# Recurrent layer: all blocks finished ahead of the output projections, and part of the elementwise work on GpSimd

## The chip, the cores and the metric

One core of a Trainium2 chip runs the whole program. The metric is the device time of one execution in microseconds, as the median of several runs.

## What is computed

Four layers, each a mixer and a squared-ReLU MLP with a residual and a layer norm, over 256 positions of 1024 features, all in float32. The mixers are a retention layer, a gated recurrent layer, an attention layer and a second retention layer. The change is in the recurrent one, layer 1:

```
gate_branch, rec = split(x @ w_in, 2)
gate_branch = gelu(gate_branch)
u = causal conv of width 4 over rec, + conv_b
r = sigmoid(blockwise u @ w_a + b_a);  i = sigmoid(blockwise u @ w_x + b_x)
log_a = -8 * r * softplus(-lam);  a = exp(log_a)
b_in = sqrt(-expm1(2 * log_a)) * (i * u)
h[t] = a[t] * h[t-1] + b_in[t]
out = (h * gate_branch) @ w_o
```

Its width is 1280, and the kernel takes it as 5 blocks of 256.

## The kernel before

Every float32 product is made of three matmuls on operands that are split into a high part (rounded to the matmul's format) and a low part (the rest): high x high, high x low, low x high (`mm3`, L145). Weights come in chunks of 1 MB. `chunk` (L122) loads one by a single DMA from SyncE's queue into one of 3 `raw` buffers and splits it into one of 5 `hl` buffers, in two halves of 1024 columns: for each, ScalarE casts the high part (L142, CAST) and VectorE subtracts for the low part (L143, TENSOR_TENSOR). A `raw` buffer is free for the next load when both halves are subtracted. An `hl` buffer is free when its matmuls are done. Activations are split in the same way. `self.hold` places low halves behind a layer norm's last step.

In the recurrent layer (`lru`, L527) the order of the work is written out by hand; a scheduler of the framework then settles the order on each engine, which the program keeps when it runs. Chunks come through a `Feed` that makes each two ahead of its use: four of `rec`, the gate weights of blocks 0 to 2, the last `rec`, then gate branch 0, the gate weights of blocks 3 and 4, gate branches 1 to 4 ("b" below) and the five projection loads ("o"). Each block n goes through these steps:
- `conv` (L569) makes U[n] from the projection in PSUM: ScalarE writes it, VectorE adds three shifted products for each half (L575). It is split into uT.
- `gates` (L579): matmuls on uT, four ScalarE functions for each half, and four VectorE steps that leave B[n] (the decay), Q[n] and U[n] (L591 to L594).
- `roots` (L607): ScalarE takes the square root of Q[n].
- `scan` (L612): VectorE multiplies U[n] by Q[n] (L613) and runs the recurrence in two scans (L615) from B[n] and U[n] into Q[n].
- `gate_branch` (L617): 48 matmuls into PSUM. Those of blocks 3 and 4 lie in two of the four work banks.
- `finish` (L621): ScalarE's gelu of the gate branch into `gg`, VectorE's product with Q[n] (L624), and the split of the product into YT[n], by ScalarE (L142) and VectorE (L143). YT has 3 buffers.
- `out` (L631): 24 matmuls of YT[n] with the projection's weights, into four accumulators.

With three buffers for YT, blocks 0 and 1 are finished right after their scans, and blocks 2, 3 and 4 behind the projections of blocks 0 and 1 (L676 to L681). `close` (L297) then does the projections of blocks 2 to 4 and the layer norm.

Of the kernel before, what the change touches and what calls it, by code (L numbers as in the profile page):

```python
# [9 lines left out]
F32 = mybir.dt.float32  # L10
F32R = mybir.dt.float32r
# [87 lines left out]
class Model:  # L99
# [19 lines left out]
        return [[self.acc.tile([128, 512], F32, name=f"acc{t}{n}", tag=f"acc{t}{n}") for n in range(2)]  # L119
                for t in range(2)]  # L120

    def chunk(self, src, k, n, pieces=2, loads=1, hold=True, mid=None):  # L122

        nc = self.nc
        raw = self.raw.tile([128, 2048], F32, name="raw", tag="raw")
        hl = self.hl.tile([128, 2, 2048], F32R, name="hl", tag="hl")
        w = k * n
        src = src.rearrange("p k n -> p (k n)")
        step = w // loads
        for a in range(0, w, step):  # L130
            nc.sync.dma_start(out=raw[:, a:a + step], in_=src[:, a:a + step])
            if mid and a == 0:
                mid()
        step = w // pieces
        for a in range(0, w, step):
            lo = self.split(hl[:, 0, a:a + step], hl[:, 1, a:a + step], raw[:, a:a + step])
            if hold and self.hold:
                self.after(lo, self.hold)
        return hl[:, :, :w].rearrange("p s (k n) -> p s k n", n=n)

    def split(self, hi, lo, x):
        self.nc.scalar.copy(out=hi, in_=x)  # L142
        return self.nc.vector.tensor_sub(out=lo, in0=x, in1=hi.bitcast(F32))  # L143

    def mm3(self, out, st, mv, start, stop):  # L145

# [380 lines left out]
    def lru(self, l, final):  # L527
        nc, mm, A, tc = self.nc, self.nc.tensor.matmul, self.A, self.tc
# [3 lines left out]
        act = nc.scalar.activation  # L532
        with tc.tile_pool(name="lru", bufs=1) as p:
            UT, GB, YT = {}, {}, {}
            U = [p.tile([128, 2, 256], F32, name=f"U{n}") for n in range(5)]
            Q = [p.tile([128, 2, 256], F32, name=f"Q{n}") for n in range(5)]
            B = [p.tile([128, 2, 256], F32, name=f"B{n}") for n in range(5)]
            last = {}

            def load(n, o, hold=True):  # L540
                return self.chunk(win[o + n], 8, 256, hold=hold)

            def block(ps, w):
                for b in range(2):
# [65 lines left out]
                last["s"] = m  # L610

            def scan(n):  # L612
                nc.vector.tensor_mul(out=U[n], in0=U[n], in1=Q[n])  # L613
                for b in range(2):
                    nc.vector.tensor_tensor_scan(out=Q[n][:, b], data0=B[n][:, b], data1=U[n][:, b], initial=0.0, op0=ALU.mult, op1=ALU.add)  # L615

# [4 lines left out]
            def finish(n):  # L621
                g = p.tile([128, 2, 256], F32, name="gg", tag="gg", bufs=2)
                self.after(act(out=g, in_=GB[n], func=AF.Gelu_apprx_tanh), last["s"])
                nc.vector.tensor_mul(out=g, in0=g, in1=Q[n])  # L624
                YT[n] = p.tile([128, 2, 2, 256], F32R, name="yT", tag="yT", bufs=3)
                self.split(YT[n][:, 0], YT[n][:, 1], g)

            def out_load(n):
                return self.chunk(wo[n], 2, 1024)

            def out(n, w, t, ns=(0, 1)):  # L631
                c = slice(t * 128, t * 128 + 128)
# [32 lines left out]
            w = feed(("b", 3))  # L665
            for n in range(5):
                roots(n)
            for n in range(5):
                scan(n)
                if n < 2:  # L670
                    finish(n)
            gate_branch(3, w)
            gate_branch(4, feed(("b", 4)))
            acc = self.accs()
            gb = self.ln_load(l, 0)
            for n in range(2):  # L676
                w = feed(("o", n))
                out(n, w, 0)
                out(n, w, 1)
                finish(n + 2)  # L680
            finish(4)  # L681
            self.close(acc, gb, final, [lambda t, ns, n=n: out(n, feed(("o", n)), t, ns) for n in (2, 3, 4)])


# [371 lines left out]
```

## Time and profile before

| | us |
|---|---|
| median of 3 runs (1320.05 to 1322.92) | 1321.05 |
| the profiled execution | 1322.59 |
| its span, first to last instruction | 1320.8 |
| TensorE busy | 1303.6 |
| VectorE busy | 956.6 |
| ScalarE busy | 658.9 |
| GpSimd busy | 26.0 |

In the rows PE is TensorE, DVE VectorE, ACT ScalarE and POOL GpSimd; L12 is line 12 of the kernel. Times in the rows below count from the start of the span, in microseconds. A row of a timeline is one instruction, or several that follow each other on the same line (x2 and so on, the whole time of the group). An instruction's time includes the end of its pipeline, so that the next one on its engine starts a little before it is over. What stands in square brackets is the idle time ahead of an instruction and what ended it. The granted clock is a share of TensorE's full speed.

### The profile page before, as it was taken

To read this page: it belongs to the slowest core of one execution; us is meant where nothing else is said; L and a number is where in the kernel's file an instruction comes from. 1 tells how busy PE (TensorE), PEld (TensorE's weight loads), DVE (VectorE), ACT (ScalarE), POOL (GpSimd) and SP (SyncE) were. 2 spreads that over 40 slices of the span, in tenths; PEclk is the share of its full clock that TensorE was granted. 3 is DMA by queue.
4 is the path that set the end of the run, shared out by engine and by line. 5 is a ranking of instruction groups with operands and counts; after the bars stand their busy time and mean duration, and the time that the engine had idled before them with its cause. 6 is when DMAs were issued, how large, how long until landed. Compare 5 with 4: busy or idle time off the path is not lost.

```text
span 1320.8 us, 17993 instructions
## 1 busy us (share of the span) xinstructions
PE 1303.6 (99%) x7130; PEld 1130.1 (86%) x7130; DVE 956.6 (72%) x1490; ACT 658.9 (50%) x1026; POOL 26.0 (2%) x40
## 2 busy tenths in 40 slices
PE   9999999999999999999999999999999999999997
PEld 6888888888889978888888888888898888888886
DVE  6976678766678988666589886666786657876664
ACT  5654445444438945444357554444444445454440
POOL 0000000000000000000010000000000000000000
PEclk9999999999999999999999999999999999999999
DMA  7745544655544366555435365555554544465540
GB/s 286 285 163 191 187 164 160 225 193 190 193 159 166 128 238 240 191 192 191 151 114 203 130 237 192 191 191 192 186 206 174 188 156 177 154 236 189 194 143 32
DMA packets 37281, 243.59 MB, mean 184 GB/s; under 512 B 4311, under 2 KB 4812, under 8 KB 10188
## 3 DMA queue, kind: packets, MB, share of 16 engines
q1 hardware_dynamic: 37196, 242.43, 51.8%
q8 instruction: 56, 0.92, 0.3%
q14 instruction: 29, 0.24, 0.1%
HBM read 241.36 MB, written 1.05 MB: 184 GB/s over the span
## 4 chain that ended last, share of the span: by engine, by line
PE 90%; DVE 5%; ACT 3%; issue 1%; DMA 0%; SPq 0%; POOL 0%; DVEq 0%; POOLq 0%; ACTq 0%
PE wk L960 14%; PE acc L148 12%; PE acc L150 12%; PE acc L149 12%; PE wk L148 10%; PE wk L150 10%; PE wk L149 10%; PE wk L962 8%; DVE hl L143 2%; PE wk L266 1%; ACT hl L142 1%; PE wk L428 1%; DMA raw<-ret_vg 0%; PE wk L984 0%; DVE Q L615 0%
## 5 line engine op out<-in xcount | busy, mean ns | idle before, releaser
L143 DVE TENSOR_TENSOR hl<-raw,hl 128x1024 fp32r<-128x1024 f32 (+3 forms) x448 | 526.3, 1196 | 176.8 <-ACT hl L142 173.8
L142 ACT CAST hl<-raw 128x1024 fp32r<-128x1024 f32 (+3 forms) x448 | 447.0, 1033 | 307.7 <-PE acc L150 174.1
L148 PE MATMUL acc<-hl,hT 128*128 128x512 f32 x512 | 200.5, 392 | 0.0
L149 PE MATMUL acc<-hl,hT 128*128 128x512 f32 x512 | 200.1, 391 | 0.0
L150 PE MATMUL acc<-hl,hT 128*128 128x512 f32 x512 | 199.2, 389 | 0.0
L960 PE MATMUL wk<-xT,hl 128*128 128x512 f32 x832 | 197.6, 390 | 0.0
L960 PEld LDWEIGHTS wk<-xT,hl 128*128 128x128 f32 x832 | 155.9, 188 | 32.3
L148 PE MATMUL wk<-hl,xT 128*128 128x512 f32 (+1 forms) x432 | 159.0, 368 | 0.3 <-ACT xT L142 0.3
L149 PE MATMUL wk<-hl,xT 128*128 128x512 f32 (+1 forms) x432 | 157.0, 364 | 0.2 <-DVE hl L143 0.2
L150 PE MATMUL wk<-hl,xT 128*128 128x512 f32 (+1 forms) x432 | 157.0, 364 | 0.0
L948 ACT COPY tb<-wk 128x256 f32<-128x256 f32 x104 | 38.8, 373 | 156.3 <-PE wk L962 156.3
L150 PEld LDWEIGHTS acc<-hl,hT 128*128 128x128 f32 x512 | 96.1, 188 | 20.3
L148 PEld LDWEIGHTS acc<-hl,hT 128*128 128x128 f32 x512 | 96.3, 188 | 18.5
L149 PEld LDWEIGHTS acc<-hl,hT 128*128 128x128 f32 x512 | 96.3, 188 | 17.9
L962 PEld LDWEIGHTS wk<-xT,hl 128*128 128x128 f32 x832 | 106.7, 191 | 4.1
L962 PE MATMUL wk<-xT,hl 128*128 128x256 f32 x832 | 107.9, 283 | 0.0
L949 DVE TENSOR_TENSOR s<-wk,tb 128x256 f32<-128x256 f32 x104 | 44.1, 424 | 80.5 <-ACT tb L948 76.8
L148 PEld LDWEIGHTS wk<-hl,xT 128*128 128x128 f32 x432 | 81.7, 189 | 14.8 <-ACT xT L142 2.6
L150 PEld LDWEIGHTS wk<-hl,xT 128*128 128x128 f32 x432 | 81.6, 189 | 14.0 <-DVE xT L143 1.6
L149 PEld LDWEIGHTS wk<-hl,xT 128*128 128x128 f32 x432 | 81.9, 190 | 12.8 <-DVE hl L143 1.1
L150 PE MATMUL wk<-xT,hl 128*128 128x256 f32 x288 | 81.6, 284 | 0.1
L148 PE MATMUL wk<-xT,hl 128*128 128x256 f32 x288 | 81.5, 283 | 0.0
(231 smaller groups left out, 1786.0 us busy)
## 6 DMA issues: line engine op xcount, KB each, us to landing
raw<-mlp SPq DMA_DIRECT2D x64, 1024.0 KB, 4.8
raw<-mlp_1b SPq DMA_DIRECT2D x56, 1024.0 KB, 4.8
raw<-ret_vg SPq DMA_DIRECT2D x30, 1024.0 KB, 4.8
raw<-ret_qk SPq DMA_DIRECT2D x16, 1024.0 KB
raw<-ret_o SPq DMA_DIRECT2D x16, 1024.0 KB, 5.0
raw<-lru_in SPq DMA_DIRECT2D x10, 1024.0 KB, 4.8
raw<-mlp_1a SPq DMA_DIRECT2D x8, 1024.0 KB
raw<-lru_o SPq DMA_DIRECT2D x5, 1024.0 KB, 4.7
```

The source lines that it names most:

```text
L142: self.nc.scalar.copy(out=hi, in_=x)
L143: return self.nc.vector.tensor_sub(out=lo, in0=x, in1=hi.bitcast(F32))
L148: mm(out, lhsT=st[0], rhs=mv[0], start=start, stop=False)
L149: mm(out, lhsT=st[0], rhs=mv[1], start=False, stop=False)
L150: mm(out, lhsT=st[1], rhs=mv[0], start=False, stop=stop)
L266: nc.tensor.transpose(ps[:, k * 128:k * 128 + 128], self.h[t][:, (j * 4 + k) * 128:(j * 4 + k + 1) * 128], self.idn)
L428: nc.tensor.transpose(tp[:, b * 128:b * 128 + 128], Y[h, t][:, b * 128:b * 128 + 128], self.idn)
L948: nc.scalar.copy(out=tb, in_=ps_lo)
L949: nc.vector.tensor_add(out=s, in0=ps_hi, in1=tb)
L960: mm(ps[b], lhsT=w[:, 0, k, f], rhs=xT[:, k], start=k == 0, stop=False)
L962: mm(ps[b][:, 256:], lhsT=w[:, 1, k, f], rhs=xT[:, k, 0], start=False, stop=k == 7)
```

## The change

The second half of a chunk's low part can be made by GpSimd (`pool=True`); it is, for the five gate-branch loads (o == 0 in `load`) and the five projection loads. GpSimd also does U*Q of blocks 1 to 4. U and B of a block become halves of one tile, UB, and YT takes its buffer from the same five slots: a block's yT is written where its U and B were. All five blocks are scanned and finished ahead of the projections, and gate branches 3 and 4 are written ahead of the scans. The lines of the changed kernel are three further on in these functions.

```
-    def chunk(self, src, k, n, pieces=2, loads=1, hold=True, mid=None):
+    def chunk(self, src, k, n, pieces=2, loads=1, hold=True, mid=None, pool=False):
...
-            lo = self.split(hl[:, 0, a:a + step], hl[:, 1, a:a + step], raw[:, a:a + step])
-            if hold and self.hold:
+            by = nc.gpsimd if pool and a + step == w else None
+            lo = self.split(hl[:, 0, a:a + step], hl[:, 1, a:a + step], raw[:, a:a + step], by)
+            if hold and self.hold and not by:
                 self.after(lo, self.hold)
...
-    def split(self, hi, lo, x):
+    def split(self, hi, lo, x, by=None):
         self.nc.scalar.copy(out=hi, in_=x)
-        return self.nc.vector.tensor_sub(out=lo, in0=x, in1=hi.bitcast(F32))
+        return (by or self.nc.vector).tensor_sub(out=lo, in0=x, in1=hi.bitcast(F32))
...
-            U = [p.tile([128, 2, 256], F32, name=f"U{n}") for n in range(5)]
+            UB = [p.tile([128, 2, 2, 256], F32, name="UB", tag="UB", bufs=5) for n in range(5)]
+            U, B = [x[:, 0] for x in UB], [x[:, 1] for x in UB]
             Q = [p.tile([128, 2, 256], F32, name=f"Q{n}") for n in range(5)]
-            B = [p.tile([128, 2, 256], F32, name=f"B{n}") for n in range(5)]
...
-                return self.chunk(win[o + n], 8, 256, hold=hold)
+                return self.chunk(win[o + n], 8, 256, hold=hold, pool=o == 0)
...
-                nc.vector.tensor_mul(out=U[n], in0=U[n], in1=Q[n])
+                (nc.gpsimd if n else nc.vector).tensor_mul(out=U[n], in0=U[n], in1=Q[n])
...
-                YT[n] = p.tile([128, 2, 2, 256], F32R, name="yT", tag="yT", bufs=3)
+                YT[n] = p.tile([128, 2, 2, 256], F32R, name="yT", tag="UB", bufs=5)
...
-                return self.chunk(wo[n], 2, 1024)
+                return self.chunk(wo[n], 2, 1024, pool=True)
...
+            gate_branch(3, w)
+            gate_branch(4, feed(("b", 4)))
             for n in range(5):
                 scan(n)
-                if n < 2:
-                    finish(n)
-            gate_branch(3, w)
-            gate_branch(4, feed(("b", 4)))
+                if n:
+                    finish(n - 1)
+            finish(4)
...
                 out(n, w, 1)
-                finish(n + 2)
-            finish(4)
```

What this does to the engines' queues is seen at three places. VectorE from the first U*Q to block 0's finished low part, before (U0 to U4, Q0 to Q4 and B0 to B4 are the blocks' tiles, gg_4143 and yT_4146 those of block 0, gg_4152 that of block 1):

```order
L613 TENSOR_TENSOR U0_3391<-U0_3391,Q0_3396 128x512
L613 TENSOR_TENSOR U1_3392<-U1_3392,Q1_3397 128x512
L615 SCALAR_TENSOR_TENSOR Q0_3396<-B0_3401,U0_3391 128x256 x2
L615 SCALAR_TENSOR_TENSOR Q1_3397<-B1_3402,U1_3392 128x256 x2
L613 TENSOR_TENSOR U2_3393<-U2_3393,Q2_3398 128x512
L613 TENSOR_TENSOR U3_3394<-U3_3394,Q3_3399 128x512
L624 TENSOR_TENSOR gg_4143<-gg_4143,Q0_3396 128x512
L624 TENSOR_TENSOR gg_4152<-gg_4152,Q1_3397 128x512
L615 SCALAR_TENSOR_TENSOR Q2_3398<-B2_3403,U2_3393 128x256 x2
L143 TENSOR_TENSOR yT_4146<-gg_4143,yT_4146 128x512
```

The same place on VectorE afterwards (hl_4185 and hl_4294 are the second and third projection loads, gg_4246 and yT_4249 block 0's):

```order
L616 TENSOR_TENSOR UB_3391<-UB_3391,Q0_3396 128x512
L618 SCALAR_TENSOR_TENSOR Q0_3396<-UB_3391 128x256 x2
L618 SCALAR_TENSOR_TENSOR Q1_3397<-UB_3392 128x256 x2
L618 SCALAR_TENSOR_TENSOR Q2_3398<-UB_3393 128x256 x2
L618 SCALAR_TENSOR_TENSOR Q3_3399<-UB_3394 128x256 x2
L146 TENSOR_TENSOR hl_4185<-raw_4184,hl_4185 128x1024
L618 SCALAR_TENSOR_TENSOR Q4_3400<-UB_3395 128x256 x2
L627 TENSOR_TENSOR gg_4246<-gg_4246,Q0_3396 128x512
L627 TENSOR_TENSOR gg_4255<-gg_4255,Q1_3397 128x512
L146 TENSOR_TENSOR hl_4294<-raw_4293,hl_4294 128x1024
L146 TENSOR_TENSOR yT_4249<-gg_4246,yT_4249 128x512
```

Block 0's low part has moved behind all ten scans and two weight halves; three U*Q that stood ahead of it, and block 4's, are gone from this queue.

GpSimd's queue in this layer afterwards (hl_4068 is gate branch 4's load, hl_4124 the first projection's; before, there is nothing between the powers of two layer norms, L166):

```order
L169 TENSOR_TENSOR rs_3380<-ve_3379,mhalf_85 128x1
L146 TENSOR_TENSOR hl_3718<-raw_3717,hl_3718 128x1024
L146 TENSOR_TENSOR hl_3891<-raw_3890,hl_3891 128x1024
L146 TENSOR_TENSOR hl_3947<-raw_3946,hl_3947 128x1024
L146 TENSOR_TENSOR hl_3983<-raw_3982,hl_3983 128x1024
L146 TENSOR_TENSOR hl_4068<-raw_4067,hl_4068 128x1024
L146 TENSOR_TENSOR hl_4124<-raw_4123,hl_4124 128x1024
L616 TENSOR_TENSOR UB_3392<-UB_3392,Q1_3397 128x512
L616 TENSOR_TENSOR UB_3393<-UB_3393,Q2_3398 128x512
L616 TENSOR_TENSOR UB_3394<-UB_3394,Q3_3399 128x512
L616 TENSOR_TENSOR UB_3395<-UB_3395,Q4_3400 128x512
L146 TENSOR_TENSOR hl_4185<-raw_4184,hl_4185 128x1024
```

The four U*Q stand behind the second half of the first projection load; three more projection halves follow.

TensorE's first matmuls of block 0's projection, before:

```order
L148 MATMUL acc00_4272<-hl_4129,yT_4146 128x512
L149 MATMUL acc00_4272<-hl_4129,yT_4146 128x512
L150 MATMUL acc00_4272<-hl_4129,yT_4146 128x512
L148 MATMUL acc01_4273<-hl_4129,yT_4146 128x512
L149 MATMUL acc01_4273<-hl_4129,yT_4146 128x512
```

And afterwards (L151 and L152 read the high part of yT, L153 the low part):

```order
L151 MATMUL acc00_4285<-hl_4124,yT_4249 128x512
L152 MATMUL acc00_4285<-hl_4124,yT_4249 128x512
L151 MATMUL acc01_4286<-hl_4124,yT_4249 128x512
L152 MATMUL acc01_4286<-hl_4124,yT_4249 128x512
L151 MATMUL acc10_4287<-hl_4124,yT_4249 128x512
L152 MATMUL acc10_4287<-hl_4124,yT_4249 128x512
L153 MATMUL acc00_4285<-hl_4124,yT_4249 128x512
```

Six matmuls on the high part alone now stand ahead of the first that reads the low part; before it was two.

## Rows read from the trace of the kernel before

**Rows 1.** The page, first part: busy us, share of the span, instructions.
```profile
span 1320.8 us, 17993 instructions
...
PE 1303.6 (99%) x7130; PEld 1130.1 (86%) x7130; DVE 956.6 (72%) x1490; ACT 658.9 (50%) x1026; POOL 26.0 (2%) x40
```

**Rows 2.** Table by stage: stretch, length, each engine's busy us, clock, DMA share, GB/s.
```profile
440.00:450.00 10.00, 10.00 (x86) 10.00 (x85) 9.37 (x14) 9.96 (x16) 0.00 (x0) 1.00 0.77 251
...
465.00:470.00 5.00, 2.91 (x13) 2.06 (x11) 4.51 (x6) 2.90 (x4) 0.00 (x0) 1.00 0.92 349
470.00:475.00 5.00, 4.73 (x14) 3.78 (x15) 3.57 (x5) 4.54 (x6) 0.00 (x0) 0.66 0.51 167
```

**Rows 3.** Timeline of TensorE: start, us, engine, line, instruction, count, idle before.
```profile
454.29 0.40 PE L148 MATMUL acc<-hl,yT 128*128 128x512 f32 x1
...
455.59 0.50 PE L150 MATMUL acc<-hl,yT 128*128 128x512 f32 x1 [0.67 <-DVE yT L143]
...
467.52 0.39 PE L148 MATMUL acc<-hl,yT 128*128 128x512 f32 x1
470.27 0.56 PE L148 MATMUL acc<-hl,yT 128*128 128x512 f32 x1 [2.36 <-ACT yT L142]
...
473.18 0.63 PE L149 MATMUL acc<-hl,yT 128*128 128x512 f32 x1
...
474.24 0.40 PE L149 MATMUL acc<-hl,yT 128*128 128x512 f32 x1
```

**Rows 4.** Timeline of VectorE over the convolutions, gates, scans and first projections.
```profile
407.93 2.42 DVE L575 SCALAR_TENSOR_TENSOR U<-rec,cols,U 128x255 f32<-128x255 f32 x6
...
436.53 1.23 DVE L143 TENSOR_TENSOR hl<-raw,hl 128x1024 fp32r<-128x1024 f32 x1 [0.58 <-ACT hl L142]
...
442.80 1.23 DVE L143 TENSOR_TENSOR hl<-raw,hl 128x1024 fp32r<-128x1024 f32 x1 [0.63 <-ACT hl L142]
...
447.42 0.42 DVE L593 TENSOR_SCALAR B<-B 128x512 f32<-128x512 f32 x1
447.75 1.28 DVE L613 TENSOR_TENSOR U<-U,Q 128x512 f32<-128x512 f32 x2
448.95 2.43 DVE L615 TENSOR_TENSOR_SCAN Q<-B,U 128x256 f32<-128x256 f32 x4
...
460.14 3.47 DVE L143 TENSOR_TENSOR hl<-raw,hl 128x1024 fp32r<-128x1024 f32 x3
```

**Rows 5.** Timeline of ScalarE from the last gate to the last finished blocks.
```profile
442.61 0.65 ACT L590 ACTIVATE tr<-tr,lr_ch 128x256 f32<-128x256 f32 x1
443.12 2.03 ACT L142 CAST hl<-raw 128x1024 fp32r<-128x1024 f32 x2
...
446.46 2.72 ACT L608 ACTIVATE Q<-Q 128x512 f32<-128x512 f32 x5
...
467.70 1.99 ACT L142 CAST hl<-raw 128x1024 fp32r<-128x1024 f32 x2 [1.05 <-DMA raw<-lru_o]
469.60 1.13 ACT L142 CAST yT<-gg 128x512 fp32r<-128x512 f32 x2
```

**Rows 6.** Timelines of GpSimd and VectorE beside two of the 36 powers.
```profile
56.51 0.56 POOL L166 TENSOR_TENSOR rs<-ve,mhalf 128x1 f32<-128x1 f32 x1 [56.06 <-DVE ve L165]
...
56.28 0.15 DVE L165 TENSOR_SCALAR ve<-mv 128x1 f32<-128x1 f32 x1
56.34 0.74 DVE L419 SCALAR_TENSOR_TENSOR y<-wk,mv,g 128x512 f32<-128x512 f32 x1
...
379.82 0.92 POOL L166 TENSOR_TENSOR rs<-ve,mhalf 128x1 f32<-128x1 f32 x1 [169.54 <-DVE ve L165]
...
379.59 1.41 DVE L292 SCALAR_TENSOR_TENSOR h<-h,mv,lng 128x512 f32<-128x512 f32 x2
```

## Prediction

> **What bounds the kernel now.** I read the page's first part first [rows 1]: TensorE is busy for 1303.6 of 1320.8 us, so any gain is a piece of TensorE time that is now lost, and the 72% of VectorE and the nearly empty GpSimd say nothing by themselves. The second view is the table by stage, over the recurrent layer, which runs from about 395 to 480 us. Up to 450 us TensorE is full; [rows 2] show the last such stretch and the two in which it loses most, and there VectorE is busy for 4.51 and 3.57 of 5 us. The third view is TensorE's queue in order of time [rows 3]. It names three losses at the start of the output projections. The first matmul of block 0's projection stands at 454.29; its third waits 0.67 us for the low part of block 0's finished output yT. At 467.52 (plus one step of 0.23) the queue stops until 470.27, 2.5 us, for the cast of block 3's yT. Behind that stop the clock is granted at half (0.66 as the mean of that stretch, [rows 2]; a matmul every 0.43 us at 473.18 against one every 0.23 at 474.24), that is 1.2 instead of 2.4 GHz: 0.34 of 5 us, 1.7 us. Together **4.9 us**. More than that this change cannot win here, since it adds and takes no matmul.
>
> Why is block 3 late? ScalarE's queue [rows 5]: the casts of the last projection weights wait 1.05 us for their transfer at 467.70, and block 3's cast stands behind them at 469.60. That transfer waits for VectorE to free a raw buffer, the second half of the second projection load, the first in the run of three at 460.14 [rows 4].
>
> **The change, part by part.** Ten second halves of weight loads (five gate-branch loads, five projection loads) leave VectorE. One lasts 1.23 us [rows 4] and, in the run of three at 460.14, follows the one before at 1.14: 11.4 us less. Four of the five U*Q leave it too, at 0.6 each (1.28 for a pair): 2.4 us. The new slots let all five finishes stand ahead of the projections, so the stop at 467.75 and its slow clock go: by then yT of blocks 2 to 4 is long queued ahead of the other weight casts. What is late next is block 0. In the order before, block 0's yT low part is written after two U*Q, four scans, two more U*Q, two products and two scans; afterwards it stands behind all ten scans, two weight halves and the products of blocks 0 and 1, and scans 1 to 4 wait for GpSimd, whose four U*Q are queued behind a weight half (the second one of the first projection load).
>
> GpSimd's price is not in this trace for such shapes. Its only work is the 128x1 power, 0.56 us where VectorE's own 128x1 instruction takes 0.15 [rows 6], 3.7 times as much. Bounds: VectorE's times, 1.23 and 0.64 us for 1024 and 512 columns, from below; 3.7 times these, 4.5 and 2.4, from above. I take the middle in ratio, 2.3 and 1.2 us, because the power is a dearer operation than a subtraction and a software start is shared by all. The Trainium skill, GPSIMD Engine Reference, section "Performance versus the Vector engine", has 4497 ns for 2048 columns; by it an estimate is 2.25 and 1.1 us, and the sum below would come out some 0.7 us lower.
>
> Do the two engines run side by side? What [rows 6] show speaks against it. The same power lasts 0.56 us beside an instruction that has one tensor in SBUF and one in PSUM (L419), and 0.92 beside one with two SBUF tensors (L292); all 16 beside L292 take 0.92, and it ends about 0.5 us after the first of the two L292 has ended. So a GpSimd read waits for a VectorE instruction with two SBUF inputs and gets in before the next one. I assume that the reverse holds too, for the time in which GpSimd reads: its price less the 0.5 us that it needs with almost nothing to read, 1.8 us for a weight half and 0.7 for a U*Q. Weight halves, scans, U*Q and products all have two SBUF inputs; the convolution steps read PSUM.
>
> The sum, with ScalarE's times kept (the change leaves its work alone):
> 1. Gate-branch halves. The first falls on a run of six convolution steps (407.93, [rows 4]) and costs nothing. Each of the other four takes 1.14 us off VectorE and shuts it out for 1.8: 4 x 0.66 = 2.6 us, less the two waits for ScalarE that VectorE has there, 0.58 and 0.63. Lag 1.4 us.
> 2. Block 4's last gate steps can start when ScalarE's tanh ends, 442.61 + 0.65 = 443.3 [rows 5]; with the lag 444.7.
> 3. From there to block 0's product VectorE's queue holds: two gate steps 1.2, a weight half 1.14, the step of 0.33 (447.42 to 447.75), U*Q 0.6, ten scans at 0.59 (2.43 for four) 5.9, a weight half 1.14, the product 0.6: 10.9 us. In between GpSimd has the second halves of two projection loads, 3.6, and four U*Q, 2.8: 6.4 us. 444.7 + 10.9 + 6.4 = 462.0.
> 4. ScalarE's cast of yT, 0.6 us (1.13 for two, [rows 5]): TensorE can start at 462.6 instead of 454.3: 8.3 us. The new order lets six matmuls run on the high part alone (1.4 us), and the low part comes 0.6 + 1.14 + 0.6 after the product, at 464.3: 0.3 more.
> 5. A stop of that length is over the 2.5 us after which the clock was halved: 1.7 us again.
> 6. Less what goes: 4.9. Sum: 8.3 + 0.3 + 1.7 - 4.9 = **+5.4 us**.
>
> The profiled execution took 1322.59 us, 1.54 above the median; so 1328.0 for it and 1326.5 against the median of 1321.05. Behind the projections nothing is paid back, because TensorE is full to the end. The buffers are no cost: the first projection load's transfer waits on GpSimd, but ScalarE asks for those casts only at 443.12.
>
> **Rivals.**
> *The engines run freely.* Then GpSimd is done with the weight half at 445.15 + 2.3 and with the four U*Q at 452.3; VectorE, released by the first root at 447.1 [rows 5], does U*Q 0.6, eight scans 4.7, a half 1.14, two scans 1.2 and the product 0.6 by 455.3. TensorE starts at 455.9: 1.6 + 0.3 - 4.9 = -3.0, **1318.0**; if the stop of 1.6 us halves the clock as well, -1.3. For it: GpSimd is empty and the earlier loads have time to spare. Against it: the 0.92 of [rows 6].
> *GpSimd shuts VectorE out for its whole instruction* (2.3 and 1.2). The lag is 4 x 1.16 - 1.2 = 3.4, GpSimd's share between 9.4: the product is ready at 467.0, TensorE starts at 467.6, 13.3 + 0.3 + 1.7 - 4.9 = +10.4, **1331.4**. This is what the Trainium skill, SBUF — State Buffer, section "Who interferes with whom", has: an exclusive lock, between a VectorE instruction with two SBUF inputs and a GpSimd one that reads SBUF, for the whole instruction. By that rule the trace agrees as far as it goes: GpSimd waited; no row shows VectorE waiting.
> *GpSimd is slow, without exclusion.* At 4.5 and 2.4 the weight half ends at 449.65, the last U*Q at 459.25, scans and product at 461.0: 7.3 + 0.3 + 1.7 - 4.9 = +4.4, **1325.5**. It decides from the point at which four U*Q behind a weight half outlast the ten scans.
> *The change does what it is for in part:* exclusion over about half the assumed time. Then steps 1 and 3 shrink to some 0.0 and 3.2, TensorE starts near 458, and 3.7 + 0.3 + 1.7 - 4.9 = +0.8: **1321.9**, no difference.
>
> **How the numbers follow.** 0.2% is 2.6 us, about what a measurement of this kernel can tell from no change. Forecast (exclusion while reading) 0.42, whole-instruction exclusion 0.14, slow GpSimd 0.08, all slower: 0.64. Half exclusion 0.15, same. Free running 0.21, of which 0.17 faster and 0.04 same because of the clock. So faster 0.17, same 0.19, slower 0.64. The range from 1318.0 to 1332.0 leaves out the lower edge of free running and a GpSimd near its upper price that also excludes.
>
> **What would show it.** VectorE's rows of 1.2 us (weight halves) stretching to about 3 beside GpSimd, and scans above 1 us, would bear out exclusion; unchanged rows beside GpSimd rows of 2 us and more, the free case. TensorE must have no wait at the fourth projection, and one long one ahead of block 0's, at 455 to 463 us. The prediction is wrong if that wait is under 2 us, or if TensorE loses time in the gates, where the trace of before has no wait, or in the layers that this diff does not touch.

## The result and the profile of the changed kernel

The changed kernel takes 1333.0 us (median) against 1321.2 for the kernel before in the same series, a ratio of 1.0090 with a 95% interval from 1.0079 to 1.0100: **11.8 us slower**. The forecast was slower by 5.4 us; the sign holds, the size forecast is less than half of the measured one, and the time lies 1 us above the range. The profiled execution took 1334.04 us, its span is 1332.3. Of 54 executions of the kernel before in the series of the experiments, the 22 with a mean granted clock of 0.999 took 1320.5 us on average and the 15 with 0.997, which is the profiled execution's, 1322.5.

The page, first part (busy us, share of the span, instructions), answers to [rows 1]. VectorE is busier than before although 14 instructions left it.

```profile
span 1332.3 us, 18016 instructions
...
PE 1304.6 (98%) x7130; PEld 1130.9 (85%) x7130; DVE 966.1 (73%) x1476; ACT 659.7 (50%) x1026; POOL 59.4 (4%) x54
```

The table by stage (stretch, length, busy us of TensorE, its weight loads, VectorE, ScalarE, GpSimd, clock, DMA share, GB/s) answers to [rows 2].

```profile
430.00:440.00 10.00, 8.29 (x67) 7.88 (x66) 9.84 (x14) 8.37 (x18) 2.40 (x1) 1.00 0.31 105
...
460.00:465.00 5.00, 0.00 (x0) 0.00 (x0) 5.00 (x8) 0.00 (x0) 0.88 (x1) 0.52 0.00 0
465.00:470.00 5.00, 1.49 (x4) 1.20 (x5) 5.00 (x7) 2.12 (x3) 0.00 (x0) 0.50 0.57 200
470.00:475.00 5.00, 5.00 (x16) 3.92 (x15) 4.94 (x5) 2.96 (x6) 2.80 (x1) 0.61 0.20 46
```

TensorE's timeline (start, length, engine, line, instruction, count, idle before) answers to [rows 3]:

```profile
439.57 0.51 PE L151 MATMUL wk<-uT,hl 128*128 128x256 f32 x2 [1.41 <-ACT uT L145]
...
457.07 0.28 PE L153 MATMUL wk<-xT,hl 128*128 128x256 f32 x1
468.51 0.80 PE L151 MATMUL acc<-hl,yT 128*128 128x512 f32 x1 [11.16 <-ACT yT L145]
...
473.37 0.63 PE L151 MATMUL acc<-hl,yT 128*128 128x512 f32 x1
...
474.52 0.40 PE L151 MATMUL acc<-hl,yT 128*128 128x512 f32 x1
...
495.63 1.03 PE L269 MATMUL wk<-idn,h 128*128 128x128 f32 x8
```

The stop at the fourth projection is gone. One stop of 11.16 us ahead of block 0's projection has taken its place, and 1.41 us (and 0.30 at 431.55) are lost in the gates. TensorE idles from 457.3; the clock is down in the stretch from 460, and behind the stop the matmuls run at the half level (one lasts 0.63 us at 473.37, 0.40 at 474.52) until 473.6. The next transposes of the layer (line 269, 266 before) stand at 495.63; in the kernel before at 484.26:

```profile
484.26 1.03 PE L266 MATMUL wk<-idn,h 128*128 128x128 f32 x8
```

That is 11.4 us, of which 0.64 were there ahead of the recurrent layer (the last power before it: 388.88 before, 389.52 after). The end of the span is as much later, so the layers that the diff doesn't touch add nothing: **10.7 us are lost between 395 and 496 us.**

Where they come from stands in VectorE's timeline, which answers to [rows 4], and in GpSimd's.

```profile
422.35 2.84 DVE L595 SCALAR_TENSOR_TENSOR Q<-UB 128x512 f32<-128x512 f32 x1
...
433.26 2.71 DVE L595 SCALAR_TENSOR_TENSOR Q<-UB 128x512 f32<-128x512 f32 x1
...
441.60 2.52 DVE L596 TENSOR_SCALAR UB<-UB 128x512 f32<-128x512 f32 x1
...
446.30 2.56 DVE L594 SCALAR_TENSOR_TENSOR UB<-e,tr 128x512 f32<-128x512 f32 x1 [0.44 <-ACT tr L593]
448.90 2.78 DVE L595 SCALAR_TENSOR_TENSOR Q<-UB 128x512 f32<-128x512 f32 x1
451.60 2.33 DVE L146 TENSOR_TENSOR hl<-raw,hl 128x1024 fp32r<-128x1024 f32 x1
453.86 1.52 DVE L596 TENSOR_SCALAR UB<-UB 128x512 f32<-128x512 f32 x1
455.30 1.78 DVE L616 TENSOR_TENSOR UB<-UB,Q 128x512 f32<-128x512 f32 x1
457.11 7.82 DVE L618 TENSOR_TENSOR_SCAN Q<-UB 128x256 f32<-128x256 f32 x8
...
467.15 1.26 DVE L627 TENSOR_TENSOR gg<-gg,Q 128x512 f32<-128x512 f32 x2
```

```profile
422.23 2.41 POOL L146 TENSOR_TENSOR hl<-raw,hl 128x1024 fp32r<-128x1024 f32 x1 [12.83 <-ACT hl L145]
433.01 2.40 POOL L146 TENSOR_TENSOR hl<-raw,hl 128x1024 fp32r<-128x1024 f32 x1 [8.37 <-DVE UB L594]
441.04 2.80 POOL L146 TENSOR_TENSOR hl<-raw,hl 128x1024 fp32r<-128x1024 f32 x1 [5.62 <-ACT hl L145]
445.90 5.23 POOL L146 TENSOR_TENSOR hl<-raw,hl 128x1024 fp32r<-128x1024 f32 x2 [2.06 <-DVE UB L597]
451.09 7.11 POOL L616 TENSOR_TENSOR UB<-UB,Q 128x512 f32<-128x512 f32 x4
458.16 2.72 POOL L146 TENSOR_TENSOR hl<-raw,hl 128x1024 fp32r<-128x1024 f32 x1
```

The gate step of line 595 (592 before) lasts 0.68 to 0.69 us alone:

```profile
445.68 0.68 DVE L592 SCALAR_TENSOR_TENSOR Q<-B 128x512 f32<-128x512 f32 x1
```

The one that starts at 422.35, 0.12 after GpSimd's weight half, lasts 2.84 and ends 0.55 after GpSimd's end: it did its own work when GpSimd had finished. The same holds at 433.26, 446.30 and 448.90, and the step of line 596 (0.41 alone) lasts 2.52. From 445.90 to 460.88 GpSimd has no gap: two weight halves, four U*Q, a third half, 15 us. VectorE's rows of these 15 us are 10.4 us longer than they are alone.

### The profile page after: what moved, and what is told of

Same layout as the page of the kernel before. It is cut to its first block, busy times and chain, and to the rows that moved or that the text cites. A ratio compares the mean times of both kernels' runs of the same rounds, so it can differ in the third digit from the quotient of the medians.

```text
span 1332.3 us, 18016 instructions
## 1 busy us (share of the span) xinstructions
PE 1304.6 (98%) x7130; PEld 1130.9 (85%) x7130; DVE 966.1 (73%) x1476; ACT 659.7 (50%) x1026; POOL 59.4 (4%) x54
## 3 DMA queue, kind: packets, MB, share of 16 engines
HBM read 241.36 MB, written 1.05 MB: 182 GB/s over the span
## 4 chain that ended last, share of the span: by engine, by line
PE 92%; DVE 5%; ACT 1%; issue 1%; DMA 1%; POOL 0%; SPq 0%; DVEq 0%; POOLq 0%
PE wk L962 14%; PE acc L151 12%; PE acc L152 12%; PE acc L153 12%; PE wk L151 10%; PE wk L153 10%; PE wk L152 10%; PE wk L964 7%; DVE hl L146 2%; PE wk L269 1%; PE wk L431 1%; DMA raw<-ret_vg 1%; DVE Q L618 0%; DVE Q L595 0%; PE wk L986 0%
## 5 line engine op out<-in xcount | busy, mean ns | idle before, releaser
L146 DVE TENSOR_TENSOR hl<-raw,hl 128x1024 fp32r<-128x1024 f32 (+3 forms) x438 | 517.1, 1203 | 178.0 <-ACT hl L145 174.8
L151 PE MATMUL acc<-hl,hT 128*128 128x512 f32 x512 | 200.5, 392 | 0.0
L152 PE MATMUL acc<-hl,hT 128*128 128x512 f32 x512 | 200.1, 391 | 0.0
L153 PE MATMUL acc<-hl,hT 128*128 128x512 f32 x512 | 199.2, 389 | 0.0
L151 PE MATMUL wk<-hl,xT 128*128 128x512 f32 (+1 forms) x432 | 159.0, 368 | 0.6 <-ACT hl L145 0.3
L152 PE MATMUL wk<-hl,xT 128*128 128x512 f32 (+1 forms) x432 | 156.8, 363 | 0.2 <-DVE hl L146 0.2
L153 PE MATMUL wk<-hl,xT 128*128 128x512 f32 (+1 forms) x432 | 157.0, 364 | 0.0
L153 PEld LDWEIGHTS acc<-hl,hT 128*128 128x128 f32 x512 | 96.2, 188 | 20.2
L151 PEld LDWEIGHTS acc<-hl,hT 128*128 128x128 f32 x512 | 96.3, 188 | 18.5
L152 PEld LDWEIGHTS acc<-hl,hT 128*128 128x128 f32 x512 | 96.3, 188 | 17.9
L151 PEld LDWEIGHTS wk<-hl,xT 128*128 128x128 f32 x432 | 81.7, 189 | 15.4 <-ACT xT L145 2.6
L153 PEld LDWEIGHTS wk<-hl,xT 128*128 128x128 f32 x432 | 81.5, 189 | 13.9 <-DVE xT L146 1.6
L152 PEld LDWEIGHTS wk<-hl,xT 128*128 128x128 f32 x432 | 81.8, 189 | 12.9 <-DVE hl L146 1.1
L153 PE MATMUL wk<-xT,hl 128*128 128x256 f32 x288 | 81.7, 284 | 0.2 <-DVE hl L146 0.2
L151 PE MATMUL wk<-xT,hl 128*128 128x256 f32 x288 | 81.5, 283 | 0.0
```

The lines of the kernel that those rows point to most:

```text
L146: return (by or self.nc.vector).tensor_sub(out=lo, in0=x, in1=hi.bitcast(F32))
L151: mm(out, lhsT=st[0], rhs=mv[0], start=start, stop=False)
L152: mm(out, lhsT=st[0], rhs=mv[1], start=False, stop=False)
L153: mm(out, lhsT=st[1], rhs=mv[0], start=False, stop=stop)
```

## The experiments

**Theory A:** a VectorE instruction with two SBUF inputs stands still while a GpSimd instruction that reads SBUF runs, for the whole of it (a hold, below), and that is the loss. **Theory B:** the new order, or the slots that U, B and yT share, makes it. The table has the medians, the ratio to the kernel before in the same series, and from the traces: where block 0's projection starts (the start-up difference, read at the last power ahead of the layer, is taken off), the sum of TensorE's waits from 400 to 490 us, and what the half clock took (busy time of each stretch of 5 us times one minus its clock). e7 and e7b are the same kernel; the time and ratio are e7's, the rest is read from e7b's trace.

| kernel | GpSimd has | us | ratio (95%) | start | waits | half clock |
|---|---|---|---|---|---|---|
| before | powers only | 1321.2 | 1 | 454.3 | 3.0 | 1.6 |
| after | 10 halves, 4 U*Q | 1333.0 | 1.0090 (1.0079 to 1.0100) | 467.9 | 12.9 | 2.7 |
| e1_order | nothing more | 1320.9 | 0.9993 (0.9985 to 1.0002) | 455.9 | 1.9 | 0 |
| e2_uq | 4 U*Q | 1326.5 | 1.0035 (1.0021 to 1.0048) | 461.3 | 6.8 | 2.5 |
| e3_gb_halves | 5 gate-branch halves | 1325.6 | 1.0030 (1.0019 to 1.0042) | 460.4 | 5.4 | 3.0 |
| e4_pr_halves | 5 projection halves | 1326.1 | 1.0035 (1.0021 to 1.0048) | 460.0 | 6.0 | 1.7 |
| e7, e7b | all, order of before | 1331.8 | 1.0075 (1.0060 to 1.0091) | 464.7 | 11.1 | 1.7 |
| e5_copy | 10 copies, 4 U*Q | 1327.2 | 1.0044 (1.0029 to 1.0059) | 462.5 | 7.5 | 2.0 |
| e6_memset | 10 fills, 4 U*Q | 1326.2 | 1.0039 (1.0024 to 1.0054) | 460.5 | 6.0 | 2.1 |
| e10_fill_only | 10 fills | 1320.7 | 0.9994 (0.9985 to 1.0004) | 456.2 | 2.3 | 1.5 |
| e8_two | 20 quarters, 4 U*Q | 1332.8 | 1.0085 (1.0069 to 1.0102) | 467.1 | 12.4 | 3.1 |
| e9_first | all, block 0 first | 1332.5 | 1.0084 (1.0069 to 1.0099) | 463.2 | 10.2 | 4.1 |
| c6_first | nothing more, block 0 first | 1321.1 | 0.9997 (0.9988 to 1.0006) | 455.0 | 2.0 | 0 |

Waits and half clock together, less the 4.6 us of the kernel before, agree with each profiled execution's difference from that of before to within 1.5 us.

**The order alone (e1).** All on VectorE:

```
-                (nc.gpsimd if n else nc.vector).tensor_mul(out=U[n], in0=U[n], in1=Q[n])
+                nc.vector.tensor_mul(out=U[n], in0=U[n], in1=Q[n])
...
-                return self.chunk(win[o + n], 8, 256, hold=hold, pool=o == 0)
+                return self.chunk(win[o + n], 8, 256, hold=hold)
...
-                return self.chunk(wo[n], 2, 1024, pool=True)
+                return self.chunk(wo[n], 2, 1024)
```

> The changed kernel's order and its shared slots, with every product and every low part back on VectorE; GpSimd has only its two powers per normalisation. Theory A (GpSimd's holds are the cause of the loss): the gates run as in the kernel before, and no wait at the fourth projection. VectorE's queue from 447.4: its rows up to block 0's product are two and a half U*Q (0.64 each), four or five scans (0.61 each), two weight halves (1.16 each), so the product ends near 456 and its low part near 458; TensorE starts block 0's projection 2 to 4 us later than 454.3 and gets 4.9 us back behind it: 1319 to 1321, that is -2 to 0 us against the kernel before. Theory B (the new order itself, or the slots that U, B and yT share, makes the loss, and GpSimd only a part): at least half of the 11.8 us stays, 1327 or more.

1320.9 us: no difference that can be measured. VectorE's and TensorE's timelines at block 0 (waits as before in brackets):

```profile
454.55 0.67 DVE L627 TENSOR_TENSOR gg<-gg,Q 128x512 f32<-128x512 f32 x1
```

```profile
455.92 0.50 PE L151 MATMUL acc<-hl,yT 128*128 128x512 f32 x1 [1.40 <-ACT yT L145]
...
457.65 0.50 PE L153 MATMUL acc<-hl,yT 128*128 128x512 f32 x1 [0.32 <-DVE yT L146]
```

Block 0's product ends at 455.2, not at 467.8; the stop of 2.4 us at the fourth projection is gone, its slow clock too. Theory B falls: order and slots by themselves make none of the loss.

**One part of GpSimd's work at a time (e2, e3, e4).** Of the diff above e2 has only the last two pieces, e3 the first and the third, e4 the first two.

> The changed kernel with only the four U*Q products on GpSimd; all low parts on VectorE. Theory A with the hold for the whole instruction: four products of 1.78 us hold VectorE's scans for 7.1 us in place of the 2.6 us that it would spend on them itself, so block 0's product comes some 4.5 us later than in the run that has the order alone: +2 to +5 us against the kernel before (1323 to 1326), and scans beside U*Q of up to 1.8 us. Were GpSimd free running: not slower than the order alone.

> The changed kernel with only the five low halves of the gate-branch weights on GpSimd; U*Q and the low halves of the projections' weights on VectorE. Theory A with the hold for the whole instruction: the last gate steps come at about 446 instead of 442.8, TensorE loses 1 to 2 us in the gates, and block 0's product comes some 3 us later than with the order alone: +1 to +5 us against the kernel before (1322 to 1326). Free running GpSimd: VectorE has 5.8 us less to do, and the time is that of the order alone or 1 to 2 us less.

> The changed kernel with only the five low halves of the projections' weights on GpSimd; U*Q and the gate branches' halves on VectorE. Theory A (hold for the whole instruction): the gates are untouched; of the five halves the one or two that run ahead of block 0's product hold VectorE's scans for about 2.4 us each in place of 1.16, those behind it run beside blocks 1 to 4, which had 2 to 4 us to spare: 0 to +3 us against the run with the order alone, 1321 to 1324. If the holds of the three groups simply add, this group's part is 1333.0 - 1320.9 less the 5.6 and 4.7 of the other two, some 2 us.

Each part alone costs 4 to 5 us against the kernel before, 5 to 5.5 against e1. e2, VectorE beside GpSimd's four U*Q:

```profile
448.98 7.40 DVE L618 TENSOR_TENSOR_SCAN Q<-UB 128x256 f32<-128x256 f32 x7
```

```profile
447.48 6.02 POOL L616 TENSOR_TENSOR UB<-UB,Q 128x512 f32<-128x512 f32 x4 [57.87 <-ACT Q L611]
```

Seven scans, three of them beside U*Q, take 7.40 us instead of seven times 0.6, 4.2. In e3 TensorE loses 1.7 us in the gates, as in the changed kernel. e4 was expected at 0 to 3 us above e1 and came out at 5. Two of its halves run ahead of block 0's product; they hold a gate step for 1.8 us and four scans for 2.2 (4.60 instead of 2.43), which are about the 4.1 us by which block 0 starts later than in e1. The half clock, 1.7 us, comes on top; the expectation had left it out.

```profile
444.96 2.49 DVE L594 SCALAR_TENSOR_TENSOR UB<-e,tr 128x512 f32<-128x512 f32 x1 [0.86 <-ACT tr L593]
...
449.76 4.60 DVE L618 TENSOR_TENSOR_SCAN Q<-UB 128x256 f32<-128x256 f32 x4
```

```profile
444.50 2.40 POOL L146 TENSOR_TENSOR hl<-raw,hl 128x1024 fp32r<-128x1024 f32 x1 [54.95 <-ACT hl L145]
450.92 2.89 POOL L146 TENSOR_TENSOR hl<-raw,hl 128x1024 fp32r<-128x1024 f32 x1 [4.02 <-ACT hl L145]
```

The parts don't add: by the ratios 5.5, 4.9 and 5.5 us over e1, 16 together, where the whole has 12.8. Each alone pays a half clock of its own, 2.5, 3.0 and 1.7 us, 7.2 in all, and the whole pays it once, 2.7. That would be 4.5 us less, more than the 3 that are missing; where the rest went is not shown.

**GpSimd's work in the order of before (e7, and e7b for its profile).**

```
-            gate_branch(3, w)
-            gate_branch(4, feed(("b", 4)))
             for n in range(5):
                 scan(n)
-                if n:
-                    finish(n - 1)
-            finish(4)
+                if n < 2:
+                    finish(n)
+            gate_branch(3, w)
+            gate_branch(4, feed(("b", 4)))
...
                 out(n, w, 1)
+                finish(n + 2)
+            finish(4)
```

> GpSimd's work of the changed kernel (all ten low halves and four U*Q) in the order of the kernel before: blocks 0 and 1 finished ahead of the last two gate branches, blocks 2 to 4 among the output projections; slots shared. Theory A: the holds cost as much as in the changed kernel, 3 to 3.5 us of lag in the gates and some 4 to 6 us at the scans, and the stop of 2.4 us at the fourth projection stays or grows: +6 to +13 us against the kernel before (1327 to 1334). Theory B (the order is the cause): within 2 us of the kernel before.

> The same kernel as GpSimd's work in the order of the kernel before, for a profile of it at full clock: the holds in the gates as in the changed kernel, last gate steps at about 446, a wait of 3 to 8 us ahead of block 0's projection and another, of some 2 us, at the fourth; 1331.8.

9.9 us slower than before, where the new order costs 12.8 over e1: the holds cost in this order too. It is the old order only as it is written. The scheduler put all ten scans ahead of block 0's product on VectorE (456.46 to 463.34), where the kernel before has four, so this pair does not separate order from holds as cleanly as e1 does. TensorE waits 7.9 us ahead of block 0's projection; of the expected second stop of 2 us only waits of up to 0.7 are there.

**What in GpSimd's work holds VectorE (e5, e6, e10).** In `split`, GpSimd copies the weight (e5) instead of subtracting, so the low part is not the difference; in e6 and e10 it fills with zeros and leaves it out, by `by.memset(lo.bitcast(F32), 0.0)` in the place of the copy. e10 has U*Q on VectorE as well.

```
-        return (by or self.nc.vector).tensor_sub(out=lo, in0=x, in1=hi.bitcast(F32))
+        if by:
+            return by.tensor_copy(out=lo, in_=x)
+        return self.nc.vector.tensor_sub(out=lo, in0=x, in1=hi.bitcast(F32))
```

> The changed kernel, in which each of GpSimd's ten half weight low parts is a copy of the weight (one input read from SBUF) instead of the difference of two; the low parts are wrong by that, and U*Q stays on GpSimd. Theory A1 (what excludes VectorE's two-input operations is that GpSimd reads SBUF at all): VectorE's operations beside a copy last as long as the copy, whatever that takes; between 1.2 and 2.6 us. Theory A2 (only two inputs on both sides collide): operations beside a copy keep their 0.68 us, and the time comes down to that of the run with U*Q alone, 1326.5, or a little above. Under A1 the time is that of the changed kernel, less 5 times what the copy is shorter, but not under 1326.

> The changed kernel, in which GpSimd fills each of its ten half weight low parts with zeros (nothing is read from SBUF) instead of making the difference; those low parts are missing by that, and U*Q stays on GpSimd. Theory A1 and A2 both: VectorE's two-input operations beside a fill keep their 0.68 us, the last gate steps are back at 443 to 444, and the time is that of the run with U*Q alone, 1326.5 +-1.5, or less, since VectorE has 11.6 us of halves less to do. Rival A3 (any work of GpSimd that touches SBUF excludes VectorE): rows of VectorE stretch to the length of the fill, and the time is between 1327 and 1333. If instead the time stayed at 1333 with rows of VectorE as short as in the kernel before, GpSimd's lateness and not the hold would be the cause.

> The changed kernel with GpSimd filling its ten half weight low parts with zeros (nothing is read from SBUF; those low parts are missing by that) and U*Q back on VectorE: GpSimd is as busy with instructions as the fill makes it, but excludes nobody from reading, and VectorE has ten halves of 1.16 us less. It shows what the change was worth without the hold. Theory A: no two-input operation of VectorE stretched, block 0's product at about 455.4, a wait of 1 to 2 us there and no other: 1318 to 1321, that is -3 to 0 us against the kernel before; the 5 us between this run and the one with U*Q on GpSimd as well (1326.2) are then the holds of U*Q alone. Rival (the instructions on GpSimd cost something else than the hold, such as the planner's order or semaphores): 1323 or more.

e5, a copy and the gate step (line 599 there, 597 in the changed kernel) that starts 0.6 us into it:

```profile
429.76 1.52 DVE L599 SCALAR_TENSOR_TENSOR UB<-ti,UB 128x512 f32<-128x512 f32 x1
```

```profile
429.16 1.58 POOL L147 CAST hl<-raw 128x1024 fp32r<-128x1024 f32 x1 [4.16 <-ACT tr L592]
```

e6, a fill beside a weight half, and two fills beside the steps of lines 598 (596 in the changed kernel) and 599:

```profile
422.84 0.90 DVE L598 TENSOR_SCALAR UB<-UB 128x512 f32<-128x512 f32 x1
424.21 0.69 DVE L599 SCALAR_TENSOR_TENSOR UB<-ti,UB 128x512 f32<-128x512 f32 x1 [0.47 <-ACT ti L593]
...
428.36 1.22 DVE L148 TENSOR_TENSOR hl<-raw,hl 128x1024 fp32r<-128x1024 f32 x1
```

```profile
422.50 2.12 POOL L147 MEMSET hl<- 128x1024 f32 x2 [9.12 <-PE wk L155]
428.89 0.95 POOL L147 MEMSET hl<- 128x1024 f32 x1 [4.26 <-PE rec L155]
```

Beside a copy, which reads one tensor, the step lasts 1.52 instead of 0.68 and ends 0.54 after it. Beside a fill, which reads none, the same step and the weight half keep their 0.69 and 1.22. So A1 holds for the three large GpSimd instructions here that read SBUF (subtraction, product, copy): they shut out VectorE's instructions with two SBUF inputs. It is the rows that tell this; e5's time alone, 1327.2, fits A2's 1326.5 "or a little above" as well. Only the step of line 598, one input and one output in SBUF, is held by the fill as well, 0.90 instead of 0.42. e10 closes the account: with GpSimd filling and U*Q on VectorE the time is 1320.7, so the 5.5 us between e10 and e6 are what U*Q on GpSimd costs. It also shows what GpSimd would have brought if its halves held no instruction with two inputs: nothing that can be measured, although VectorE has ten halves of 1.14 us less to do. Block 0's product still comes at 455.25: VectorE waits 0.94 us for ScalarE's first root and then takes four U*Q and four scans of other blocks and a weight half ahead of the product. TensorE waits 1.75 and 0.52 us for block 0, and the half clock takes 1.5; of these the expectation had only the first.

**For how long (e8).** Each half in two instructions of 512 columns.

```
+            m = x.shape[-1] // 2
+            by.tensor_sub(out=lo[:, :m], in0=x[:, :m], in1=hi.bitcast(F32)[:, :m])
+            return by.tensor_sub(out=lo[:, m:], in0=x[:, m:], in1=hi.bitcast(F32)[:, m:])
```

> The changed kernel, each of GpSimd's half weight low parts made by two instructions of 512 columns instead of one of 1024. Theory A (a two-input operation of VectorE waits for the end of the GpSimd instruction that is running, then goes ahead of GpSimd's next): no operation of VectorE in the gates lasts above 2 us (0.68 + some 1.2) where the changed kernel has five of 2.5 to 2.84; VectorE and GpSimd take turns, and the last gate steps come 0 to 2 us earlier than 446.3: 1330 to 1333. Rival (GpSimd keeps the port as long as it has work queued): rows of VectorE of 2.5 to 3 us as before, and the time of the changed kernel.

VectorE's and GpSimd's timelines at the second gate-branch half (lines 599 and 600 are 595 and 596 of the changed kernel):

```profile
421.22 1.72 DVE L599 SCALAR_TENSOR_TENSOR Q<-UB 128x512 f32<-128x512 f32 x1
422.86 0.47 DVE L582 SCALAR_TENSOR_TENSOR UB<-rec,cols,UB 128x253 f32<-128x253 f32 x1
423.25 1.13 DVE L600 TENSOR_SCALAR UB<-UB 128x512 f32<-128x512 f32 x1
```

```profile
421.09 1.29 POOL L148 TENSOR_TENSOR hl<-raw,hl 128x512 fp32r<-128x512 f32 x1 [12.68 <-ACT hl L145]
422.34 1.75 POOL L149 TENSOR_TENSOR hl<-raw,hl 128x512 fp32r<-128x512 f32 x1
```

The gate step runs when the first instruction has ended, GpSimd's second takes 0.46 longer than its first, and the next VectorE step waits for that one in turn; the convolution step between them, which reads PSUM, keeps its 0.47. The hold on VectorE is one instruction long here, and it is mutual. Gate steps stay under 1.75 us; weight halves, 1.22 alone, take 2.3, which the expectation had overlooked. As much time is lost in smaller pieces: 1332.8 us.

**Block 0 first (e9, c6).** On VectorE the scans of blocks 1 to 4 are put behind block 0's product (e9, from the changed kernel); c6 is e1 with U*Q of blocks 2 to 4 and block 1's second scan behind it. Both call `finish(n)` right behind `scan(n)`.

```
-                    nc.vector.tensor_tensor_scan(out=Q[n][:, b], data0=B[n][:, b], data1=U[n][:, b], initial=0.0, op0=ALU.mult, op1=ALU.add)
+                    m = nc.vector.tensor_tensor_scan(out=Q[n][:, b], data0=B[n][:, b], data1=U[n][:, b], initial=0.0, op0=ALU.mult, op1=ALU.add)
+                    if n:
+                        self.after(m, last["g"])
...
-                nc.vector.tensor_mul(out=g, in0=g, in1=Q[n])
+                g0 = nc.vector.tensor_mul(out=g, in0=g, in1=Q[n])
+                last.setdefault("g", g0)
```

> The changed kernel with all of GpSimd's work as it is, but VectorE takes block 0's product and its finish ahead of the scans of blocks 1 to 4 (in the changed kernel eight scans, 7.8 us, two more scans and a weight half stand ahead of it). Theory A splits the changed kernel's loss in two: holds ahead of block 0's first product (U*Q of block 0 at 455.3 instead of 447.2), which this run keeps, and the queue between that and block 0's finished product, 11.8 us there, about 5 here: the product ends at 461 to 462, TensorE starts block 0's projection at 462 to 463 instead of 468.5, and the time is 1326 to 1328.5. If the holds did not matter and the order did it all, the time would be that of the order alone, 1321.

> The order alone (all on VectorE), and block 0 put first on VectorE: U*Q of blocks 2 to 4 and the second scan of block 1 are issued behind block 0's product. In the run with the order alone that product stands at 454.55 behind three scans and an U*Q of other blocks, and TensorE waits 1.4 + 0.3 us for block 0. Here the product ends at 453.6 instead of 455.2, its cast waits for a weight cast on ScalarE until 454.45, and TensorE starts block 0's projection at 455.2 instead of 455.9: 0.7 to 1.7 us less than the order alone, 1319.2 to 1320.2, and 1.5 to 2.5 us under the kernel before.

e9's block 0 starts at 463.5, half a microsecond behind what was expected, and the time doesn't follow, 1332.5. TensorE and GpSimd, and VectorE's low part of yT:

```profile
463.47 0.80 PE L151 MATMUL acc<-hl,yT 128*128 128x512 f32 x1 [6.50 <-ACT yT L145]
...
467.93 0.80 PE L153 MATMUL acc<-hl,yT 128*128 128x512 f32 x1 [1.96 <-DVE yT L146]
...
473.64 0.42 PE L151 MATMUL acc<-hl,yT 128*128 128x512 f32 x1
```

```profile
465.04 2.84 DVE L146 TENSOR_TENSOR yT<-gg,yT 128x512 fp32r<-128x512 f32 x1
```

```profile
464.50 2.83 POOL L146 TENSOR_TENSOR hl<-raw,hl 128x1024 fp32r<-128x1024 f32 x1 [4.00 <-issue]
```

The next weight half holds the low part, TensorE stops again for 1.96 us, and the clock stays at the half level until 473.6, as in the changed kernel: 4.1 us instead of 2.7. Of the 5 us by which TensorE started earlier, 2.0 and 1.4 go back so, and the rest is the 1.4 us between the spans (1330.9 and 1332.3). The expectation had priced neither. c6 starts block 0 at 455.2 with a wait of 0.5, as expected, but gives the gain back at the last projections, where weight halves come 0.6 us late, and at the next layer's input (0.9 us at 487.0): VectorE's queue is full up to there, and what is put first makes something else last. No version beats the kernel before by more than can be measured.

## Why the prediction was right in sign and wrong in size

*What bounds, and what can be won.* The stop at the fourth projection and its clock went with the order, as step 6 has it (e1). But of the 4.9 us e1 keeps only 1.9 by the spans of the profiled executions and 0.9 by the medians, which is not told from zero. Block 0's new waits take 1.7 of them back; 1.3 us stays unaccounted for. The profiled execution of before stood 1.5 us above its median and has a mean clock of 0.997, the lower of the two named with the result. So the 1.7 us of clock in the 4.9 may not be lost in every execution; no trace of another one shows whether it is.

*GpSimd's price.* 2.3 and 1.2 us were taken (the middle in ratio of 1.23 and 4.5 is 2.35). In the changed kernel halves last 2.4 to 2.8; a U*Q lasts 1.5 (e2) to 1.78 on average. A piece of 512 columns that meets nobody takes 1.29 (e8). The lower ends are near the values taken; what is above them fits with VectorE holding GpSimd, which e8 shows. The estimate of 2.25 us for 1024 columns worked out from the Trainium skill (GPSIMD Engine Reference, section "Performance versus the Vector engine") is 0.15 below the shortest row, 2.40.

*Steps 1 and 2, the lag in the gates.* Block 4's last gate steps start at 446.30, 445.7 without the start-up difference, against 444.7: 1 us off. The lag didn't stay on VectorE. The hold at 433.26 passes through the convolution and the cast to TensorE, which stops for 1.41 us at 439.57, and from there to ScalarE's tanh, for which VectorE then waits (0.44 at 446.30). The prediction let VectorE's two waits soak up 1.2 us of it; and it named a loss of TensorE in the gates as a sign against itself, which is there.

*Step 3 is the one that failed.* From the last gate steps to block 0's product it had 10.9 us of VectorE's own work and 6.4 us of holds. The own work is right; 446.30 to 467.75 is 21.45 us, so the holds are 10.5. Three terms were too small. First, the hold of a half, 1.8: line 594 is 1.9 and line 595 2.1 us longer than alone, and so is, by 2.1, the second of the eight scans, which meets the half at 458.16:

```profile
458.67 2.76 DVE L618 TENSOR_TENSOR_SCAN Q<-UB 128x256 f32<-128x256 f32 x1
```

Second, the count: three halves stand in that stretch and not two, because the fifth gate-branch half, entered in step 1, ran only at 445.90, beside block 4's gate steps. So 6.1 instead of 3.6. Third, U*Q: four at 0.7 were 2.8; the weight half at 451.60, line 596, block 0's U*Q and the first scan are 1.0 to 1.1 us longer each beside them, 4.3. Of the 4 us that are missing, the third half is 2 and the size of the holds the other 2. Behind the size is the assumption that GpSimd shuts VectorE out only while it reads, its price less 0.5 us. The head start is not a share in which both run: the VectorE step at 422.35 waited to the end of a GpSimd instruction that had begun 0.12 us before it.

*Steps 4 and 5.* TensorE starts at 468.5, 467.9 on the clock of before, against 462.6 (455 to 463 among the signs): the 5.1 us of steps 2 and 3 and 0.2 for the cast. The extra wait for the low part (0.3) isn't there. The half clock takes 2.7 us, not 1.7: behind a stop of 11 us it stays for 5.1 us of work (468.51 to 473.6). From block 0's start to the transposes the changed kernel needs 27.1 us and the kernel before 30.0, so 2.9 us come back where 4.9 less 2.7 was to be expected; the other 0.7 is not traced. The prediction's own terms give 2.9 as well (4.9 less 0.3 and 1.7), which is luck. Sum: 13.6 - 2.9 = 10.7. So all that the sum missed in the layer, 5.3 us, lies ahead of block 0's start.

*The rivals.* Whole-instruction exclusion had 1331.4 and a chance of 0.14. It is what happens beside weight halves and U*Q: last gate steps 446.7 (445.7 measured, less the start-up difference), product 467.0 (467.1), start 467.6 (467.9). That the last two agree so well is luck: its lag was 1.0 us too long, and its 9.4 us of holds, with two halves instead of three, 1.1 too short. Of the 1.6 us by which its time is low, 0.3 are in the layer and 0.6 ahead of it; most of the rest is that the profiled execution of before stood 1.5 us above its median and that of the changed kernel 1.05. This is the rule of the Trainium skill, SBUF — State Buffer, section "Who interferes with whom": an exclusive lock for the whole instruction, between a VectorE instruction with two SBUF inputs and a GpSimd one that reads SBUF, not one that only writes it. This case's traces agree on these points: 2.84 us instead of 0.68 beside a half, 1.52 beside a copy, 0.69 beside a fill, 0.47 for the step that reads PSUM. They don't agree beside the power: it reads SBUF too, and the pair of L292 that it meets lasts 1.41 us [rows 6], no longer than the pair of L293 right behind, which begins when GpSimd has ended:

```profile
380.91 1.41 DVE L293 SCALAR_TENSOR_TENSOR h<-h,rs,lnb 128x512 f32<-128x512 f32 x2
```

So the rows of before did speak for a hold shorter than the rule's, as the prediction has it; what they show of a 128x1 instruction did not carry over to 128x512 and 128x1024. The free-running rival had 1318.0 at 0.21; the nearest to it that could be run, e10, took 1320.7: U*Q is on VectorE there, and the order's wait at block 0 is in it, the slow clock as well. Slow GpSimd without exclusion falls with VectorE's own rows, which it would have left at their length, and exclusion over half the time with the same rows.

## What to carry to other kernels

In this kernel elementwise work that goes from a full VectorE to GpSimd relieves nothing where both read SBUF: in the 15 us in which GpSimd worked without a gap VectorE lost 10.4 us to be rid of 5.8 (three halves of 1.14, four U*Q of 0.6). It cost nothing beside VectorE instructions that read PSUM (the half at 406.8). No run here was made to show the same beside an idle VectorE. A stop that a new order removes is worth at most what is next in the same engine's queue: here 4.9 us shrank to 0.9, and putting one block first (e9, c6) only moved the wait.

## What the hardware showed beyond that

- The step with one SBUF input (lines 596, 598) is held too, even by a fill: 0.90 instead of 0.42 us (0.93 in e10), and 2.52 beside a half. The prediction had counted on two-input instructions only.
- The hold is mutual: GpSimd's second piece of 512 columns lasts 1.75 where the first has 1.29 (e8). It can be much longer on GpSimd's side. In e9 a projection half lasts 8.16 us; seven VectorE instructions follow each other beside it at their usual 0.68 and 1.21 us, and it ends 2.3 us after the last of them. Why GpSimd got no turn between them, as it did elsewhere, is not shown.

```profile
472.52 8.16 POOL L146 TENSOR_TENSOR hl<-raw,hl 128x1024 fp32r<-128x1024 f32 x1 [5.20 <-ACT hl L145]
```

- After stops of 11.2, 6.8 and 3.7 us (changed kernel, e2, e3) TensorE came back at 1.2 GHz; after 1.4 and 0.3 us (e1) at 2.4. In e10 it came back at 2.4 after 1.75 and 0.52 us, and fell to 1.2 with matmuls running, from about 459 to 462. How soon the clock came back didn't depend on the start alone: with a second stop (e9) work begun 5 us earlier reached the full level at the same 473.6.
